# Seven products of sums in the up-projection of a diffusion-transformer layer's MLP

## The chip, the cores and the metric

The kernel runs on one core of a Trainium2 chip. The metric is the device time of one launch in microseconds (us). Engines are called as in the profile: PE (TensorE: matmuls), PEld (its weight loads), DVE (VectorE), ACT (ScalarE), POOL (GpSimd), SP (SyncE, which issues nearly all DMAs of this kernel).

## The reference, cut to what matters

One layer over 2048 tokens of width 1024: modulated norm, input projection, retention and grouped attention side by side, output projection, then an MLP with a squared ReLU, and a final norm.

```python
h = _modulate(_rmsnorm(x, norm1_g), sh1, sc1)
...
x = x + g1 * (jnp.concatenate([ret, att], axis=-1) @ w_out)
h2 = _modulate(_rmsnorm(x, norm2_g), sh2, sc2)
x = x + g2 * (jnp.square(jax.nn.relu(h2 @ w_ff1)) @ w_ff2)
...
return _rmsnorm(x, final_norm_g)
```

`h2` is 2048 x 1024, `w_ff1` 1024 x 4096, `w_ff2` 4096 x 1024, all in 32-bit floats. The change is in how `h2 @ w_ff1` (the up-projection) is computed.

## The kernel before, in words

**Three stages.** First the projections of the normed input, in an order that a scheduler chooses at build time; at the end of this stage `ff_scales` works out powers of two by which weights and activations of the MLP are scaled. Then attention, with retention and the output projection woven into it. Then the MLP, called feed-forward here. Attention and feed-forward are ordered by hand: attention is a list of numbered steps, each with phases ("scores", "exp", "late", "dma" and so on), and `on(k, phase, fn)` puts a call into step k. There are 18 steps for each of 32 groups of attention. Within each engine the instructions run in the order in which they were called, and so do the DMAs of SP.

**16-bit halves.** In feed-forward every operand is held as two 16-bit floats, hi and lo: ACT writes hi as a cast, DVE (or POOL) writes lo as the difference (`split16`, and the same with a scale in `make_piece`). A product of two such operands takes three matmuls: hi by hi, hi by lo, lo by hi.

**The output tiles.** `output_tile(t, ...)` adds the output projection of token tile t (128 tokens) to x, stores the row (`x1_d`), norms it, transposes it and stores the modulated, transposed tile of `h2` in DRAM (`h2_d[t]`: 128 partitions x 8 slices of the width x 128 tokens). The tiles come from the last token to the first, one per 24 steps; the last one or two end after attention.

**Feed-forward.** The 2048 tokens are taken in two halves (`halves`) of 8 tiles. For each half the 4096 hidden columns are taken in 16 blocks of 256, so there are 32 blocks. A block has two parts:
- Up: 4 tiles (two slices f of 128 hidden columns by two groups tg of 512 tokens). A tile is 8 slices of the width x 3 matmuls of 128 x 128 by 512, into one of four PSUM banks (`up_part`). `up_out` then takes it: ReLU with scale (ACT), square (POOL), hi (ACT), lo (DVE).
- Down: 16 tiles (8 token tiles m by two slices n of 512 columns), each of 2 x 3 matmuls (`down`); DVE adds each to the row `acc` of its token tile. There are four banks for these, two pools of two, taken by turns: m even and m odd; in the first block only one pool.

The weights of a block come in pieces of 256 KB (`fetch_piece`) and are split, w2 after a multiplication by the gate g2 on POOL (`make_piece`), one block ahead. The h2 of a half stays in SBUF as hi and lo: `fetch_h` reads 16 pieces, `make_h` splits them. `prelude` puts this for the first half, and the up tiles of block 0, into the last steps of attention. At the turn between the halves, block 15's down tiles are interleaved with the second half's splits, and with the squares, roots, final scaling and stores of the first half's rows, for which the second half's rows are then loaded (`ending`, steps kept in the list `rest`).

Of the kernel before, what the change touches and what calls it, by code (L numbers as in the profile page):

```python
# [54 lines left out]
def layer_kernel(ctx: ExitStack, tc: tile.TileContext, a: dict, out: bass.AP):  # L55
# [43 lines left out]
    x1_d = scratch("x1", NT, [P, D])  # L99
    gate_d = [dram.tile([D], F32, name=f"gate{r}", tag=f"gate{r}") for r in range(2)]  # L100
# [12 lines left out]
    w2s = const.tile([P, 1], F32, name="w2s")  # L113
# [146 lines left out]
    with ExitStack() as st:  # L260
# [400 lines left out]
        def ff_scales():  # L661
# [3 lines left out]
            def spread():  # L665
                w = xp.tile([P, D], F32, name="fs", tag="x", bufs=6)
                x["m"], m = w[:, 4:516], w[:, :4]
                nc.vector.tensor_reduce(
# [11 lines left out]
            def scales():  # L680
                b = sm.tile([P, 8], F32, name="fsb", tag="fsb", bufs=1)
# [13 lines left out]
                nc.vector.tensor_scalar_mul(b[:, 6:7], b[:, 6:7], 8192.0)  # L695
# [4 lines left out]
                nc.vector.tensor_scalar_mul(sc1, sc1, 8192.0)  # L700
# [4 lines left out]
                nc.vector.scalar_tensor_tensor(scu, scu, 2.0**-26, b[:, 7:8], op0=ALU.mult, op1=ALU.mult)  # L705

                nc.vector.reciprocal(w2s, w2)
                nc.vector.tensor_scalar_mul(w2s, w2s, 8192.0)
# [211 lines left out]
    xp = pool(side, "wx", 2, side="right")  # L920
# [253 lines left out]
    def output_weights(k0):  # L1174
# [8 lines left out]
        def fetch(k, n):  # L1183
            w = xp.tile([P, 2, 512], F32, name="wos", tag="xr")
# [33 lines left out]
    def output_tile(t, k, direct, first, last):  # L1218
# [6 lines left out]
        def fetch_x():  # L1225
            y["x"] = xp.tile([P, D], F32, name="xr", tag="xr")
            nc.sync.dma_start(y["x"], a["x"][0, t * P : (t + 1) * P, :])
# [102 lines left out]

    for i in range(3):
        on(18 + i, "begin", more_keys, 0, i)
        on(26 + 4 * i, "late", more_keys, 1, i)
    done = attention()
    k = output_weights(retention(24))
    for n, t in enumerate(range(NT - 1, -1, -1)):
# [4 lines left out]
        made_at, last = output_tile(t, k, n >= DIRECT, n == 0, n == NT - 1)  # L1341

# [5 lines left out]
    halves = [list(range(NT - 1, NT // 2 - 1, -1)), list(range(NT // 2 - 1, -1, -1))]  # L1348
    ff = {}
    w1, w2 = {}, {}  # L1350
# [3 lines left out]
    def open_early():  # L1354
        attn.close()
        keep.close()
        ff["h"] = pool(early_ff, "fh")
        ff["w1"] = pool(early_ff, "fw", 6)
        ff["s"] = pool(early_ff, "fs", 5)
        ff["ps1"] = pool(early_ff, "fp1", 4, space=PSUM)  # L1360

    def open_late():
        room.close()
        ff["w2"] = pool(late_ff, "fw2", 3, side="right")
        ff["r"] = pool(late_ff, "fr", 2, side="right")
        ff["up"] = pool(late_ff, "fq", 6, side="right")
# [6 lines left out]
        nc.sync.dma_start(ff["g2"], gate_d[1].partition_broadcast(P))  # L1373

        m = one.tile([P, 4], F32, name="gm")
        e, r, k = (m[:, i : i + 1] for i in range(3))
        nc.vector.tensor_reduce(e, ff["g2"], axis=AX.X, op=ALU.max, apply_absolute_value=True)
        binade(e)
        nc.vector.tensor_scalar_mul(e, e, 2.0)
        nc.vector.reciprocal(r, e)  # L1380
        nc.vector.tensor_scalar_mul(r, r, w2s)
        nc.vector.tensor_scalar_mul(ff["g2"], ff["g2"], r)
        nc.vector.tensor_tensor(k, sc2, e, op=ALU.mult)
        ff["k"] = k
# [5 lines left out]
    def pieces(b):  # L1390
        return [(2, b, 1, 0), (2, b, 1, 1), (1, b + 1, 0), (1, b + 1, 1), (2, b + 1, 0, 0), (2, b + 1, 0, 1)] + [
            (1, b + 1, 2),
            (1, b + 1, 3),
        ]

    queue = [(1, 0, i) for i in range(4)] + [(2, 0, 0, n) for n in range(2)]
    for b in range(2 * NB):
        queue += [p for p in pieces(b) if p[1] < 2 * NB]
    fetched, made = [], []

    def fetch_piece():
        if len(fetched) == len(queue):
            return
        m, b, i, *n = queue[len(fetched)]
        f0 = b % NB * FB
        w = ff["s"].tile([P, 512], F32, name="ws", tag="ws")
        if m == 1:
            src = a["w_ff1"][0, 2 * i * P : (2 * i + 2) * P, f0 : f0 + FB]
            nc.sync.dma_start(w.rearrange("p (k n) -> p k n", k=2), src.rearrange("(k p) n -> p k n", p=P))
        else:  # L1410
            c = slice(n[0] * 512, (n[0] + 1) * 512)
            nc.sync.dma_start(w, a["w_ff2"][0, f0 + i * P : f0 + (i + 1) * P, c])
        fetched.append(w)

    def make_piece(ahead=2):
        if len(made) == len(queue):
            return
        while len(fetched) < min(len(made) + 1 + ahead, len(queue)):
            fetch_piece()
        m, b, i, *n = queue[len(made)]  # L1420
        w = fetched[len(made)]
        made.append(None)
        if m == 1:
            hi = ff["w1"].tile([P, 2, FB], F16, name="w1hi", tag="w1hi")
            lo = ff["w1"].tile([P, 2, FB], F16, name="w1lo", tag="w1lo")
            w1[b, i] = hi, lo
            w = w.rearrange("p (k n) -> p k n", k=2)
            nc.scalar.activation(hi, w, AF.Copy, scale=sc1)
            nc.vector.scalar_tensor_tensor(lo, w, sc1, hi, op0=ALU.mult, op1=ALU.subtract)
        else:  # L1430
            if n[0] == 0:
                w2[b, i] = [ff["w2"].tile([P, D], F16, name=f"w2{x}", tag=f"w2{x}") for x in ("hi", "lo")]
            c = slice(n[0] * 512, (n[0] + 1) * 512)
            hi, lo = w2[b, i]
            nc.gpsimd.tensor_tensor(w, w, ff["g2"][:, c], op=ALU.mult)
            split16(hi[:, c], lo[:, c], w)

    def new_h():
        ff["hs"] = [
            [ff["h"].tile([P, KT, 512], F16, name=f"h2{x}", tag=f"h2{x}{tg}") for x in ("hi", "lo")]  # L1440
            for tg in range(2)
        ]

    def fetch_h(hf, i):

        u = ff["u", i] = ff["s"].tile([P, 4, P], F32, name="u", tag="ws")
        nc.sync.dma_start(u, h2_d[halves[hf][i // 2]][:, i % 2 * 4 : i % 2 * 4 + 4])

    def make_h(i, eng=None):
        j, q = i // 2, i % 2  # L1450
        hi, lo = (x[:, 4 * q : 4 * q + 4, j % 4 * P : (j % 4 + 1) * P] for x in ff["hs"][j // 4])
        split16(hi, lo, ff.pop(("u", i)), eng or (nc.vector if i % 2 else nc.gpsimd))


    UP = [(f, tg) for tg in range(2) for f in range(NF)]
# [3 lines left out]
    def up_part(b, f, tg, k):  # L1459
        if k == 0:  # L1460
            pu[f, tg] = ff["ps1"].tile([P, 512], F32, name="pu", tag="pu")
        ps = pu[f, tg]
        whi, wlo = (x[:, k % 2, f * P : (f + 1) * P] for x in w1[b, k // 2])
        hi, lo = (x[:, k] for x in ff["hs"][tg])
        mm(ps, whi, hi, start=k == 0, stop=False)  # L1465
        mm(ps, whi, lo, start=False, stop=False)  # L1466
        mm(ps, wlo, hi, start=False, stop=k == KT - 1)  # L1467

    def up_out(f, tg):
        r = ff["r"].tile([P, 512], F32, name="r", tag="r")  # L1470
# [230 lines left out]
```

## Time and profile before

| | |
|---|---|
| median of 3 runs | 3048.44 us (3046.94 to 3048.74) |
| the profiled execution | 3047.53 us, span 3045.7 us |
| mean granted TensorE clock | 0.986 |
| PE busy, share of the span | 94% |
| DVE, ACT, POOL busy | 63%, 43%, 42% |
| DMA moved | 317.48 MB, mean 104 GB/s |
| feed-forward's matmuls (32 blocks x 192) | 6144 of 17524 |
| first up matmul, first down matmul, last down matmul start at | 1680.2, 1707.5, 3033.4 us |

The span is the time from the first to the last instruction of the profiled execution; its own time is a little longer. A stretch from A to B is counted in us from the span's start. Busy time of PE is the time in which at least one matmul was under way. In a timeline's row stand the start, the duration, engine, line, operation, the tiles written and read, the form, how many were merged, and in brackets the idle time of that engine just before, with what ended it.

### The profile page before, as it was taken

How to read it: one execution, taken by the hardware profiler on the slowest of the kernel's cores; microseconds unless marked ns; L12 is line 12 of the kernel's file. 1: busy time of each engine (PE TensorE's matmuls, PEld its weight loads, DVE VectorE, ACT ScalarE, POOL GpSimd, SP SyncE). 2: the span in 40 equal slices, each digit the busy share in tenths (PEclk: the TensorE clock that was granted, in tenths of full speed). 3: DMA queues.
4: the chain of work that ended last, by engine and by line, in shares of the span. 5: the costliest groups of instructions: out<-in, count | busy, mean ns of one | idle time of the engine just before them, and what ended most of it. 6: DMA issues, size and time to landing. Idle time of an engine off the chain costs nothing.

```text
span 3045.7 us, 45858 instructions
## 1 busy us (share of the span) xinstructions
PE 2874.4 (94%) x17524; PEld 1740.0 (57%) x17524; DVE 1932.4 (63%) x3035; ACT 1295.5 (43%) x2120; POOL 1271.7 (42%) x1046
## 2 busy tenths in 40 slices
PE   7999898998888799999998999999999999999998
PEld 3777787776666566666666444444444444444443
DVE  5889657449888977777775555554555555555455
ACT  2343334236667577777777322222223322222222
POOL 2536346236787655555555412222224321222222
PEclk9999999999999899999999999999999999999999
DMA  8988643435233212211112511111112411111111
GB/s 291 337 299 284 213 134 106 132 99 169 86 113 105 73 56 67 68 61 61 61 51 80 192 49 51 49 52 52 56 49 93 163 52 49 52 49 52 53 52 56
DMA packets 212116, 317.48 MB, mean 104 GB/s; under 512 B 49460, under 2 KB 110132, under 8 KB 211896
## 3 DMA queue, kind: packets, MB, share of 16 engines
q1 hardware_dynamic: 201616, 307.06, 30.5%
q10 hardware_dynamic: 10280, 7.48, 0.8%
q8 instruction: 138, 2.26, 0.3%
q14 instruction: 82, 0.67, 0.1%
HBM read 254.56 MB, written 59.91 MB: 103 GB/s over the span
## 4 chain that ended last, share of the span: by engine, by line
PE 69%; DVE 14%; DMA 6%; POOL 4%; issue 4%; ACT 2%; SPq 0%; ACTq 0%; DVEq 0%; POOLq 0%
PE pd L1482 7%; PE pd L1484 7%; PE pd L1483 7%; PE pu L1467 7%; PE pu L1465 7%; PE pu L1466 7%; PE o L229 3%; PE st L196 3%; PE st L195 3%; PE mp L158 3%; PE pso L789 3%; DVE nm L171 2%; PE pso L791 2%; PE pso L790 2%; PE bank L1250 2%
## 5 line engine op out<-in xcount | busy, mean ns | idle before, releaser
L1472 POOL TENSOR_TENSOR r<-r 128x512 f32<-128x512 f32 x128 | 134.5, 1051 | 942.2 <-ACT r L1471 942.2
L171 DVE TENSOR_REDUCE nm<-mp 128x1 f32<-128x512 f32 (+1 forms) x576 | 391.4, 685 | 210.9 <-PE mp L158 176.1
L1485 DVE SCALAR_TENSOR_TENSOR acc<-pd,gm,acc 128x512 f32<-128x512 f32 x512 | 373.7, 746 | 154.0 <-PE pd L1484 153.8
L212 POOL TENSOR_TENSOR plo<-p,phi 128x1024 f16<-128x1024 f32 x160 | 368.8, 2305 | 226.2 <-ACT phi L205 195.8
L201 ACT ACTIVATE p<-st 128x512 f32<-128x512 f32 x576 | 340.7, 598 | 249.2 <-PE st L196 174.5
L71 DVE TENSOR_TENSOR ulo<-r,uhi 128x512 f16<-128x512 f32 x128 | 111.4, 870 | 460.4 <-ACT uhi L70 460.4
L1482 PE MATMUL pd<-w2hi,uhi 128*128 128x512 f16 x1024 | 390.0, 381 | 14.1 <-DVE acc L1485 13.9
L1466 PE MATMUL pu<-h2lo,w1hi 128*128 128x512 f16 x1024 | 388.7, 380 | 2.6 <-POOL h2lo L71 2.6
L1465 PE MATMUL pu<-h2hi,w1hi 128*128 128x512 f16 x1024 | 388.9, 380 | 1.2 <-ACT h2hi L70 1.2
L1483 PE MATMUL pd<-w2lo,uhi 128*128 128x512 f16 x1024 | 389.9, 381 | 0.0
L1484 PE MATMUL pd<-w2hi,ulo 128*128 128x512 f16 x1024 | 389.7, 381 | 0.1
L1467 PE MATMUL pu<-h2hi,w1lo 128*128 128x512 f16 x1024 | 388.7, 380 | 0.0
L70 ACT ACTIVATE w2hi<-ws 128x512 f16<-128x512 f32 x128 | 77.4, 627 | 557.4 <-PE pd L1484 484.1
L789 PE MATMUL pso<-whi,hi_l 128*128 128x512 f32 (+1 forms) x768 | 295.1, 386 | 10.1 <-ACT xs L524 5.4
L205 ACT ACTIVATE phi<-p 128x1024 f16<-128x1024 f32 x288 | 303.7, 1055 | 0.0
L791 PE MATMUL pso<-whi,lo_l 128*128 128x512 f32 (+1 forms) x768 | 292.1, 381 | 3.3 <-DVE lo_l L67 3.3
L790 PE MATMUL pso<-wlo,hi_l 128*128 128x512 f32 (+1 forms) x768 | 291.5, 379 | 3.1 <-DVE wlo L67 3.1
L158 PE MATMUL mp<-ks,qr 128*128 128x512 f16 x512 | 196.7, 384 | 55.8 <-DVE nm L171 55.6
L229 PE MATMUL o<-wv,phi 128*128 128x129 f16 x2304 | 244.1, 221 | 0.0
L228 PE MATMUL o<-wv,plo 128*128 128x65 f16 x2304 | 237.2, 194 | 5.8 <-DVE plo L214 4.9
L228 PEld LDWEIGHTS <-plo 128*128 128x128 f16 x2304 | 203.1, 98 | 53.7 <-issue 37.5
L214 DVE TENSOR_TENSOR plo<-p,phi 128x512 f16<-128x512 f32 x256 | 214.4, 839 | 19.2 <-ACT phi L205 19.1
(357 smaller groups left out, 5409.2 us busy)
## 6 DMA issues: line engine op xcount, KB each, us to landing
ws<-in_w_ff SPq DMA_DIRECT2D x256, 256.0 KB, 2.7
wm<-in_w_ff SPq DMA_DIRECT2D x64, 512.0 KB, 5.5
wst<-in_w_in SPq DMA_DIRECT2D x60, 512.0 KB, 5.3
wst<-in_w_mod SPq DMA_DIRECT2D x32, 512.0 KB, 5.9
orv<-rv SPq DMA_DIRECT2D x35, 256.0 KB, 3.0
ork<-rk SPq DMA_DIRECT2D x34, 256.0 KB, 3.0
wst<-in_w_mod SPq DMA_DIRECT2D x32, 256.0 KB, 4.4
x_l<-in_x SPq DMA_DIRECT2D x16, 512.0 KB, 7.5
```

The lines of the kernel that those rows point to most:

```text
L171: nc.vector.tensor_reduce(dst, src, axis=AX.X, op=ALU.max, negate=True)
L212: nc.gpsimd.tensor_tensor(lo, p, hi, op=ALU.subtract)
L228: mm(o[:, : HD + 1], lo[:, i, c], v[:, : HD + 1], start=False, stop=False)
L789: mm(ps[:, :width], hi[:, k], wh, start=k == 0, stop=False)
L791: mm(ps[:, :width], lo[:, k], wh, start=False, stop=k == KT - 1)
L1465: mm(ps, whi, hi, start=k == 0, stop=False)
L1466: mm(ps, whi, lo, start=False, stop=False)
L1467: mm(ps, wlo, hi, start=False, stop=k == KT - 1)
L1482: mm(ps, uh, wh, start=f == 0, stop=False)
L1483: mm(ps, uh, wl, start=False, stop=False)
L1484: mm(ps, ul, wh, start=False, stop=f == NF - 1)
L1485: nc.vector.scalar_tensor_tensor(acc[:, c], ps, ff["k"], acc[:, c], op0=ALU.mult, op1=ALU.add)
```

## The change

**Seven products.** With the width cut in two halves (first and last four slices), the block's 256 columns in two slices f, and the 1024 tokens of a half in two groups tg, the up-projection of a block is a 2 x 2 by 2 x 2 block product. It is now computed as seven products of sums of blocks, each of 4 slices x 3 matmuls, and `up_out` puts the four tiles together from them as they come: product 0 is copied out of PSUM by ACT, each later one is added by DVE to a running sum in SBUF; after products 3, 4, 5 and 6 one of the four tiles is complete, and ReLU and square follow; `up_split` (hi, lo) of a tile is called one product later (`SPLIT_AFTER`), the last one after the first down tile.

**Weight forms.** `fetch_w1` reads a block's 1 MB of w1 in two DMAs into two 4 KB rows per partition, two blocks ahead. `sum_w1` makes four sums on POOL, `form_w1` splits seven forms (hi on ACT, lo on DVE) during the seven products of the block before (for block 1: during the first seven down tiles of block 0).

**h2 forms.** `h_pair` takes two token tiles (one of each tg), makes four differences on POOL, splits seven forms, and stores each in DRAM (`hf_d`), in runs of 256 bytes; a half has four such pairs. Those of the first half are put into the attention steps after output tiles 11 to 8, those of the second half between the down tiles with even m from block 1 on, one step each (52 in all). `fetch_h` reads the seven forms of a half, 1 MB each, in one DMA each.

**Order of the down tiles.** Outside of the turn and the last block, the four tiles of m = 6 and 7 of a block are kept back until after the next block's seven products (`LATE`).

**Scales.** The scaling of g2, before at the start of feed-forward, is done in `ff_scales` in the projection stage, and read back from DRAM (`gs_d`). The steps of the powers of two change with it.

The diff, cut to its core:

```diff
+    hf_d = [scratch(f"hf{i}", 7, [P, 2, 4, 512], F16) for i in range(2)]
+    gs_d = dram.tile([D], F32, name="gs", tag="gs")
...
+    def h_pair(hf, j):
+        x = {}
+        def fetch(g):
+            w = xp.tile([P, KT, P], F32, name="hb", tag="hb", bufs=2)
+            nc.sync.dma_start(w, h2_d[halves[hf][j + 4 * g]])
+            x[f"b1{g + 1}"], x[f"b2{g + 1}"] = w[:, :4], w[:, 4:]
+        def add(to, p, q, at=None):
+            x[to] = x[at] if at else xp.tile([P, 4, P], F32, name="hs", tag="hu", bufs=3)
+            nc.gpsimd.tensor_tensor(x[to], x[p], x[q], op=ALU.subtract)
+        def form(i, w):
+            f = xp.tile([P, 2, 4, P], F16, name="hp", tag="hp", bufs=2)
+            split16(f[:, 0], f[:, 1], x[w])
+            nc.sync.dma_start(hf_d[hf][i][:, :, :, j * P : (j + 1) * P], f)
...
+        if t in halves[0][4:]:
+            for i, step in enumerate(h_pair(0, 11 - t)):
+                on(last + 2 + 2 * i, "dma" if i < 2 else "late", step)
...
+    def form_w1(b, i):
+        w = w1[b, i] = ff["w1"].tile([P, 2, 4, P], F16, name="w1f", tag="w1f")
+        src = raw1[b, FORMS1[i]]
+        nc.scalar.activation(w[:, 0], src, AF.Copy, scale=sc1)
+        nc.vector.scalar_tensor_tensor(w[:, 1], src, sc1, w[:, 0], op0=ALU.mult, op1=ALU.subtract)
...
-    UP = [(f, tg) for tg in range(2) for f in range(NF)]
-    def up_part(b, f, tg, k):
+    def up_part(b, i, k):
         if k == 0:
-            pu[f, tg] = ff["ps1"].tile([P, 512], F32, name="pu", tag="pu")
-        ps = pu[f, tg]
-        whi, wlo = (x[:, k % 2, f * P : (f + 1) * P] for x in w1[b, k // 2])
-        hi, lo = (x[:, k] for x in ff["hs"][tg])
-        mm(ps, whi, hi, start=k == 0, stop=False)
-        mm(ps, whi, lo, start=False, stop=False)
-        mm(ps, wlo, hi, start=False, stop=k == KT - 1)
+            pu[i] = ff["ps1"].tile([P, 512], F32, name="pu", tag="pu")
+        whi, wlo = (w1[b, i][:, x, k] for x in range(2))
+        hi, lo = (hs[i][:, x, k] for x in range(2))
+        mm(pu[i], whi, hi, start=k == 0, stop=False)
+        mm(pu[i], whi, lo, start=False, stop=False)
+        mm(pu[i], wlo, hi, start=False, stop=k == 3)
...
-    def up_out(f, tg):
-        r = ff["r"].tile([P, 512], F32, name="r", tag="r")
-        nc.scalar.activation(r, pu.pop((f, tg)), AF.Relu, scale=scu)
+    def relu(f, tg):
+        r = rs[f, tg]
+        nc.scalar.activation(r, r, AF.Relu, scale=scu)
         nc.gpsimd.tensor_tensor(r, r, r, op=ALU.mult)
+    def up_out(i):
+        ps = pu.pop(i)
+        def add(to, x):
+            nc.vector.tensor_tensor(to, ps, x, op=ALU.add)
+            return to
+        if i == 0:
+            pu["v"] = new_r("v")
+            nc.scalar.activation(pu["v"], ps, AF.Copy)
+        elif i == 1:
+            pu["q"] = add(new_r("q"), pu["v"])
+        elif i == 2:
+            rs[1, 0] = add(new_r("w"), pu["q"])
+        elif i == 3:
+            rs[0, 0] = add(new_r("r"), pu["v"])
+            relu(0, 0)
+        elif i == 4:
+            pu["w"] = rs[1, 0]
+            rs[1, 0] = add(new_r("r"), pu["w"])
+            relu(1, 0)
+        elif i == 5:
+            rs[1, 1] = add(pu["w"], pu["w"])
+            relu(1, 1)
+            add(pu["q"], pu["q"])
+        elif i == 6:
+            rs[0, 1] = add(pu["q"], pu["q"])
+            relu(0, 1)
+    SPLIT_AFTER = {4: (0, 0), 5: (1, 0), 6: (1, 1), 7: (0, 1)}
...
+        pairs = [step for j in range(4) for step in h_pair(1, j)]
+        LATE = (6, 7)
         for b in range(2 * NB):
...
+            jobs = [("up", i) for i in range(7) if b]
+            if b % NB:
+                jobs += [("down", b - 1, m, n) for m in LATE for n in range(2)]
+            jobs += [("down", b, m, n) for m in range(NM) for n in range(2) if turn or final or m not in LATE]
             for i, (what, *at) in enumerate(jobs):
                 if what == "up":
+                    for k in range(4):
+                        up_part(b, i, k)
+                    up_out(i)
+                    if i in SPLIT_AFTER:
+                        up_split_of(b, *SPLIT_AFTER[i])
+                    if b < 2 * NB - 1:
+                        if i < 4:
+                            sum_w1(b + 1, *SUMS1[(0, 1, 2, 3)[i]])
+                        form_w1(b + 1, i)
+                    if turn:
+                        fetch_h(1, i)
...
+                bb, m, n = at
+                if b and i == 8:
+                    up_split_of(b, *SPLIT_AFTER[7])
+                down(bb, m, n, accs[m])
...
+                if pairs and b and m % 2 == 0:
+                    pairs.pop(0)()
```

More of the change, by code (lines that the diff above doesn't have):

```diff
@@ L1415, in make_piece, with fetch_w1 @@
[L1415 to L1420, printed above, removed]
+    raw1, w1, w2, hs = {}, {}, {}, {}
+    def fetch_w1(b):
+        f0 = b % NB * FB
+        for i in range(2):
+            w = xp.tile([P, D], F32, name="w1r", tag="xr", bufs=3).rearrange("p (k n) -> p k n", k=4)
+            src = a["w_ff1"][0, i * 512 : (i + 1) * 512, f0 : f0 + FB]
+            nc.sync.dma_start(w, src.rearrange("(k p) n -> p k n", p=P))
+            for j in range(2):
+                raw1[b, f"a{j + 1}{i + 1}"] = w[:, :, j * P : (j + 1) * P]
@@ new lines, in layer_kernel, with fetch_w2, make_w2 @@
+    queue2 = [(b, i, n) for b in range(2 * NB) for i in range(NF) for n in range(2)]
+    fetched, made = [], []
+    def fetch_w2():
+        if len(fetched) < len(queue2):
+            b, i, n = queue2[len(fetched)]
+            f0 = b % NB * FB
+            w = ff["s"].tile([P, 512], F32, name="ws", tag="ws")
+            c = slice(n * 512, (n + 1) * 512)
+            nc.sync.dma_start(w, a["w_ff2"][0, f0 + i * P : f0 + (i + 1) * P, c])
+            fetched.append(w)
+    def make_w2(ahead=2):
+        if len(made) == len(queue2):
+            return
+        while len(fetched) < min(len(made) + 1 + ahead, len(queue2)):
+            fetch_w2()
+        b, i, n = queue2[len(made)]
```

218 lines of the change are left out of this document (85 added, 133 removed).

## The prediction

> **What bounds the kernel now.** I read the page first (span, shares), then the stretches of the span, then the instructions of the feed-forward stretch by form, then the timeline of single engines there.
>
> ```profile
> span 3045.7 us, 45858 instructions
> ## 1 busy us (share of the span) xinstructions
> PE 2874.4 (94%) x17524; PEld 1740.0 (57%) x17524; DVE 1932.4 (63%) x3035; ACT 1295.5 (43%) x2120; POOL 1271.7 (42%) x1046
> ...
> ```
>
> The profiled execution took 3047.53 us, 1.8 us more than its span; the median of the three runs shown is 3048.44, 0.9 us above it. The sum below is made against 3047.5. A measurement of this kernel tells about 0.2% (6 us) from no change.
>
> The page says TensorE; whether it has slack has to be read by stretch. Columns below: stretch, length, busy time and count of PE, PEld, DVE, ACT, POOL, then granted clock, DMA share, GB/s.
>
> ```profile
> 1300.00:1400.00 100.00, 98.33 (x872) 66.96 (x871) 72.02 (x124) 73.79 (x117) 54.06 (x35) 1.00 0.21 66
> 1680.00:1710.00 30.00, 26.15 (x113) 11.51 (x112) 14.81 (x23) 12.85 (x23) 16.27 (x15) 0.94 0.82 279
> 1790.00:2200.00 410.00, 410.00 (x1901) 185.89 (x1900) 208.49 (x279) 98.56 (x158) 95.60 (x77) 1.00 0.16 51
> 2337.00:2400.00 63.00, 52.35 (x221) 22.36 (x220) 39.12 (x44) 28.15 (x50) 35.48 (x30) 0.92 0.67 238
> 2400.00:3000.00 600.00, 600.00 (x2781) 272.01 (x2780) 304.51 (x406) 142.72 (x228) 140.39 (x113) 1.00 0.15 49
> ```
>
> In both long feed-forward stretches PE is busy to the last digit, with 600 us / 2781 = 0.2158 us for a matmul. A block has 96 up and 96 down matmuls: 192 x 0.2158 = 41.4 us. The ReLU of the last up tile comes back after just that (2002.60 and 2044.04 in the ACT rows below), so nothing but PE sets a block, and a matmul less is 0.2158 us less, for as long as the other engines keep up. The places where PE loses time are the stretch at 1680 (3.9 us idle), where feed-forward begins, and the turn between the halves of the sequence: 63.0 - 221 x 0.2158 = 15.3 us.
>
> **Part 1: the matmuls.** Seven products of 4 x 3 matmuls replace 4 tiles of 8 x 3: 84 for 96. Moving width (512) and weight shape stay. 32 blocks x 12 x 0.2158 = **-82.9 us**, if every block stays bound by PE.
>
> **Part 2: what the seven products leave for VectorE.** Before, a finished tile goes PSUM, ReLU (ACT), square (POOL), hi (ACT), lo (DVE), once in 5.2 us (24 x 0.2158). Now a product ends every 12 x 0.2158 = 2.59 us, and most need an add on DVE ahead of the ReLU; beside each product DVE also makes one of seven weight forms' low parts (four before). Durations (busy us, mean ns of one):
>
> ```profile
> L1485 DVE SCALAR_TENSOR_TENSOR acc<-pd,gm,acc 128x512 f32<-128x512 f32 x208 | 152.2, 746 | 66.4 <-PE pd L1484 66.4
> ...
> L1472 POOL TENSOR_TENSOR r<-r 128x512 f32<-128x512 f32 x53 | 55.0, 1038 | 410.6 <-ACT r L1471 410.6
> ...
> L1429 DVE SCALAR_TENSOR_TENSOR w1lo<-ws,sc,w1hi 128x512 f16<-128x512 f32 x52 | 37.6, 744 | 0.0
> L1471 ACT ACTIVATE r<-pu,scu 128x512 f32<-128x512 f32 x53 | 36.2, 682 | 113.8 <-PE pu L1467 113.8
> L1428 ACT ACTIVATE w1hi<-ws,sc 128x512 f16<-128x512 f32 x52 | 34.3, 706 | 0.0
> L70 ACT ACTIVATE uhi<-r 128x512 f16<-128x512 f32 x52 | 32.7, 630 | 59.7 <-POOL r L1472 59.7
> ```
> ```profile
> 1999.99 0.69 DVE L71 TENSOR_TENSOR ulo<-r,uhi 128x512 f16<-128x512 f32 x1 [1.66 <-ACT uhi L70]
> 2005.10 1.08 DVE L71 TENSOR_TENSOR ulo<-r,uhi 128x512 f16<-128x512 f32 x1 [4.42 <-ACT uhi L70]
> 2006.10 2.71 DVE L1485 SCALAR_TENSOR_TENSOR acc<-pd,gm,acc 128x512 f32<-128x512 f32 x4
> ```
> ```profile
> 2002.60 0.69 ACT L1471 ACTIVATE r<-pu,scu 128x512 f32<-128x512 f32 x1 [2.64 <-PE pu L1467]
> 2004.44 0.63 ACT L70 ACTIVATE uhi<-r 128x512 f16<-128x512 f32 x1 [1.15 <-POOL r L1472]
> ...
> 2044.04 0.69 ACT L1471 ACTIVATE r<-pu,scu 128x512 f32<-128x512 f32 x1 [2.64 <-PE pu L1467]
> ```
> ```profile
> 2003.37 1.04 POOL L1472 TENSOR_TENSOR r<-r 128x512 f32<-128x512 f32 x1 [4.07 <-ACT r L1471]
> 2004.37 2.94 POOL L1435 TENSOR_TENSOR ws<-ws,g2b 128x512 f32<-128x512 f32 x2
> ```
> ```profile
> 1678.59 0.68 DVE L1256 TENSOR_TENSOR xr<-bank,xr 128x512 f32<-128x512 f32 x1
> ```
>
> Total load is no worry: 7 adds, 7 form lows, 4 u lows, 16 evacuations and 4 w2 lows at about 0.7 are 27 us of DVE in 39. The order is. From the fifth product on, DVE's queue reads: add, u low of the tile before, form low, next add. ACT's reads: ReLU of this tile, u hi of the tile before, form hi. So the u low waits for a u hi that stands behind this product's ReLU, which waits for this product's add. One turn of that ring: add 0.69, about 0.08 to hand over, ReLU 0.61 until ACT takes the next (0.69 less a 0.08 overlap), u hi 0.63, 0.03, u low 0.60 to 0.99 (the 0.69 and 1.08 above, less overlap; the long one ran while POOL multiplied), form low 0.66: **3.30 to 3.69 us, against 2.59 that PE needs**. I take 3.45: POOL's square overlaps about half of the u low.
>
> Count from T, the end of the fifth product. Its add starts at about T+0.35 (0.2 to 0.5, behind the fourth product's form low). Three rings later, behind the sixth's and seventh's, the queue comes to the first down tile's evacuation: 0.35 + 3 x 3.45 + 0.75 = T+11.45. What PE does meanwhile: products six and seven, then the four down tiles kept back from the block before (they hide the last splits), into the four banks. The fifth down tile wants the first one's bank at 2 x 2.59 + 4 x 1.295 - 0.17 = T+10.19 (a down tile is 6 matmuls, 1.295 us; a matmul is shown 0.38 long though one starts each 0.2158, so an end is seen 0.17 after the next start). So PE waits **1.26 us** there (ends 0.66 and 2.13). Before, the same place has little room too: the last up tile is visible at 2002.57, DVE's u low stalls for u hi till 2005.10, the first evacuation ends at 2006.85, and the fifth down tile is due 4 x 1.295 - 0.17 = 5.01 later, at 2007.58. 30 blocks have this sequence: +37.8 us (0.66 gives 20, 2.13 gives 64; 0 if I have the order's effect wrong). After the stall DVE gains 1.295 - 0.66 a tile and is level by the next block.
>
> On the u low, the Trainium skill (SBUF — State Buffer, "Who interferes with whom") says that a VectorE instruction with two SBUF inputs and a GpSimd one exclude each other for the whole instruction. The rows show a share, not a lock: the u low at 2005.10 ended at 2006.18, while POOL's two multiplications were at work from 2004.37 to 2007.31. Had the first of them (half of 2.94, to 2005.84) kept it out, it would have ended no sooner than 2006.53. What a lock would give is rival B.
>
> **Part 3: forms of h2.** Each half has 4 pairs x 7 forms (hi on ACT, lo on DVE, one store) and 4 differences on POOL per pair. First half: inside attention, about 98 steps, some 160 us by my estimate. It adds 28 x 0.63 = 18 us ACT, 28 x 0.8 = 22 us DVE, 16 x 1.04 = 17 us POOL, lifting 74, 72 and 54% by 11 to 14 points; none reaches PE's 98%, but each form makes DVE wait for ACT in the middle of its maxima, on which PE waits. Taken at +3 (0 to 10). Second half: 52 steps, 8 a block, from block 1 on, between down tiles, right where DVE is behind; two buffers make a form wait for the store before last. The stores stand in SP's queue and wait there for DVE; behind them are q loads (first half) and w2 loads, both issued some tiles ahead. +1.5 us in 6.5 blocks, **+10** (0 to 26).
>
> **Part 4: start and turn.** The split of h2 (16 pieces a half) goes; instead seven tiles of 1.05 MB are read per half: 7.3 MB at 279 GB/s (row of 1680) is 26 us. At the start their products are spread over the last output tile's, so PE needs them at a pace of 4 us and is spared the 3.9 us idle; the last tile's x row now stands behind five of them in SP's queue, some 5 us late, and DVE with it, which the four up banks cover; but w2 still comes behind, and the first down tile needs u and w2, due about where it is now (1707.5, below). Block 0 has two down banks, and now seven forms beside its first seven tiles. Together **+2** (-5 to +10).
>
> ```profile
> L1482 PE MATMUL pd<-w2hi,uhi x1024: 376/379/634, 1707.5 to 3033.4; 128*128 128x512 f16 x171
> ```
>
> At the turn the loads go out as each product of the last block frees its tile, and 16 down tiles (20.7 us) and four late ones cover them. What stays is DVE finishing the first half's rows between evacuations, so of the 15.3 us I take off only **-4** (-9 to +3).
>
> ```profile
> 2354.79 0.58 PE L1482 MATMUL pd<-w2hi,uhi 128*128 128x512 f16 x1 [3.31 <-DVE acc L1485]
> ...
> 2360.59 0.38 PE L1482 MATMUL pd<-w2hi,uhi 128*128 128x512 f16 x1 [1.39 <-DVE acc L1485]
> ```
>
> These two rows show Part 2's wait as it exists now, PE idle until DVE empties a bank. The gate and scale work moved into the projection stage (one reduction, one scaling, a load, a store) lies beside its matmuls: +0.5 (0 to 3).
>
> **Sum.** -82.9 + 37.8 + 3 + 10 + 2 - 4 + 0.5 = -33.6: **3014 us**. Its own range, with the stall between 0.66 and about 1.6 and the smaller terms moving together, is 2990 to 3036.
>
> **Rivals.**
> A, DVE keeps up (overlaps I don't see): stall 0, second-half forms +3: -82.9 + 3 + 3 + 2 - 4 + 0.5 = -78, 2969 us. For it: DVE is at 51% in the row of 2400. Against: the ring is counted from rows.
> B, the ring is longer. If POOL's square locks the u low out until it ends (0.5 us later), the ring is 3.85, the stall 0.35 + 11.55 + 0.75 - 10.19 = 2.46, 30 of them 74 us; with the second half's forms at +20 the change is -82.9 + 74 + 20 + 3 + 2 - 4 + 0.5 = +13: **3060, slower**. It decides from a ring of about 3.8. This is the result of the skill's lock.
> C, the waits cool the clock. After the 3.31 us gap a matmul takes 0.58, after 1.39 us 0.38; so stalls of 1.3 should not. If they do, the turn's clock (0.92 over 63 us, 5 us for two episodes, 2.5 each) prices 30 of them at 75: 3089. The Trainium skill (TensorE: Matmul & The Clock Gate, "A second HAM failure mode: psum-queue depth-cycling") warns of just such short idles between groups; the 0.38 row speaks against it here.
> D, the 7.3 MB are not hidden: 26 us against the 18.1 of 84 matmuls, 8 us at either end, and no gain at the turn: about 3034.
>
> **How the numbers follow.** Forecast 0.52, A 0.20, B 0.15, C 0.05, D 0.08. Predicted 3014. The range 2968 to 3050 takes in A's value, D and the part of B near break-even; some 0.08 lies below it and 0.12 above. Faster by over 0.2%: forecast, A and D, 0.80. B's short end gives 0.04 within 0.2% and C 0.01: 0.05. Slower: 0.15.
>
> **What would show it.** Right: matmul count down by 384; last ReLUs of successive blocks some 40.1 us apart (38.9 under A, over 41.4 under B); one PE gap a block of about 1.3 us ahead of the fifth down tile, released by DVE's accumulation; DVE's adds at 3.4 to 3.5 us in products five to seven; larger gaps in blocks 1 to 7. Attention's end within 10 us of now. Wrong: no gaps, gaps released by a DMA, or matmuls of 0.58 after each gap.

## The result, and the profile after

| | before | after |
|---|---|---|
| median of 4 runs, same chip | 3047.69 us | 3137.59 us (3136.97 to 3138.87) |
| the profiled execution's span | 3045.7 us | 3136.2 us |
| mean granted TensorE clock | 0.986 | 0.971 |

The changed kernel is slower: ratio 1.0296 (95% interval 1.0278 to 1.0314). The forecast was 3014 us, its range ended at 3050; the measured time is 88 us beyond that. Medians leave out one run of experiment 8 (5785.31 us) and two of experiment 12 (8578.34 and 13887.15 us), slow ones at a granted clock of 1.0 whose cause stays open. (DVE is VectorE, POOL is GpSimd, ACT is ScalarE.) On the page of after 384 matmuls are indeed gone, and PE's share of the span has fallen all the same:

```profile
span 3136.2 us, 45423 instructions
PE 2841.7 (91%) x17140; PEld 1710.7 (55%) x17140; DVE 2233.8 (71%) x3399; ACT 1388.2 (44%) x2272; POOL 1487.9 (47%) x1182
...
L1541 PE MATMUL pd<-w2hi,uhi 128*128 128x512 f16 x1024 | 405.1, 396 | 115.5 <-DVE acc L1544 105.0
```

PE waits 105 us for VectorE's evacuations ahead of down tiles. The stretches that the prediction read as "PE busy to the last digit", and the stretch of attention with the first half's h2 forms, after (stretch, length, then PE, PEld, DVE, ACT, POOL, clock, DMA share, GB/s):

```profile
1270.00:1450.00 180.00, 161.95 (x1393) 107.89 (x1392) 156.00 (x228) 133.94 (x219) 114.97 (x75) 1.00 0.42 123
1790.00:2200.00 410.00, 377.86 (x1680) 167.11 (x1680) 299.79 (x388) 129.70 (x211) 176.94 (x130) 0.96 0.26 79
2470.00:3077.00 607.00, 562.58 (x2517) 249.53 (x2516) 401.91 (x533) 176.15 (x280) 217.66 (x165) 0.97 0.14 46
```

Feed-forward has idle time and a clock below 1. The same amount of attention, counted by matmuls, before:

```profile
1270.00:1432.00 162.00, 158.71 (x1390) 107.39 (x1389) 118.71 (x201) 119.00 (x191) 89.09 (x58) 1.00 0.22 69
```

So 1390 matmuls of attention take 180 us where they took 162, with VectorE 37 us busier.

**A block.** Blocks (first up matmul to the next block's) took 41.44 us before, away from the start and the turn. After, in the second half of the tokens, they take 43.8 to 44.0 in most cases and 42.48 in four of fourteen (in the first half 42.4 to 44.1, and 47.4 in block 3); 180 x 0.2158 would be 38.85. PE's rows at the fifth down tile of the block that begins at 2469.7:

```profile
2492.84 0.38 PE L1543 MATMUL pd<-w2hi,ulo 128*128 128x512 f16 x1
2496.31 0.38 PE L1541 MATMUL pd<-w2hi,uhi 128*128 128x512 f16 x1 [3.09 <-DVE acc L1544]
2496.52 0.49 PE L1542 MATMUL pd<-w2lo,uhi 128*128 128x512 f16 x1
2496.81 0.63 PE L1543 MATMUL pd<-w2hi,ulo 128*128 128x512 f16 x1
2497.23 0.63 PE L1541 MATMUL pd<-w2hi,uhi 128*128 128x512 f16 x1
2497.66 0.63 PE L1542 MATMUL pd<-w2lo,uhi 128*128 128x512 f16 x1
```

It is the one gap that was forecast, at the place and with the releaser forecast, and 3.25 us long (start to start, less 0.2158; the bracket shows 3.09 since a matmul's end is seen late), not 1.26. Behind it some eight matmuls start 0.43 us apart: the clock has halved (its record is in the last section), 1.6 us more. In a block of 42.48 us the same gap is followed by full speed:

```profile
2583.88 0.38 PE L1541 MATMUL pd<-w2hi,uhi 128*128 128x512 f16 x1 [3.09 <-DVE acc L1544]
2584.10 0.38 PE L1542 MATMUL pd<-w2lo,uhi 128*128 128x512 f16 x1
2584.31 0.38 PE L1543 MATMUL pd<-w2hi,ulo 128*128 128x512 f16 x1
```

The chain that leads to this gap (start, length, what; "issue" is time in which the engine waits for nothing that the profile records):

```profile
2483.40 0.69 DVE r L1507
...
2485.45 0.65 DVE ulo L71
2486.09 0.39 issue
2486.48 0.74 DVE w1f L1441
2487.22 0.61 DVE w L1507
...
2490.91 0.61 DVE q L1507
...
2492.82 0.68 DVE ulo L71
2493.49 0.36 issue
2493.85 0.29 DVE w1f L1441
2494.14 1.38 issue
2495.52 0.75 DVE acc L1544
```

It is the ring of the prediction, add, ReLU, u high, u low, form low, but with unexplained time inside the u low (0.36 to 0.39) and 1.38 us inside the last form's low. GpSimd's rows, and the whole durations on VectorE, say what stands there:

```profile
2492.34 1.04 POOL L1496 TENSOR_TENSOR q<-q 128x512 f32<-128x512 f32 x1 [2.64 <-ACT q L1495]
2493.34 1.71 POOL L1468 TENSOR_TENSOR ws<-ws,g2b 128x512 f32<-128x512 f32 x1
```
```profile
2492.82 1.11 DVE L71 TENSOR_TENSOR ulo<-w,uhi 128x512 f16<-128x512 f32 x1 [1.31 <-ACT uhi L70]
2493.85 1.75 DVE L1441 SCALAR_TENSOR_TENSOR w1f<-w1s,sc,w1f 128x512 f16<-128x512 f32 x1
2495.52 0.74 DVE L1544 SCALAR_TENSOR_TENSOR acc<-pd,sc,acc 128x512 f32<-128x512 f32 x1
```

The square ends at 2493.38, and the u low 0.55 later; the multiplication, which could start at 2493.34, ends at 2495.05, 1.12 after the u low (begun with no low of VectorE running, it takes 1.27); the form's low ends another 0.55 later (alone it takes 0.74). Each waits for the other to finish. The evacuation, which reads PSUM, takes its plain 0.74 although GpSimd goes on multiplying.

**Where the 90 us are**, on the profiled executions, from the starts of matmuls and of attention's exponentials:

| part | forecast | measured |
|---|---|---|
| 384 matmuls fewer | -82.9 | -82.9 |
| waits in blocks 1 to 15 and 17 to 30 (gaps 102, slow matmuls 35) | +47.8 | +137.5 |
| attention with the first half's h2 forms | +3 | +19.0 |
| start of feed-forward, block 0 | +2 | +19.4 |
| turn | -4 | -5.6 |
| projection, last block | +0.5 | +2.8 |
| sum | -33.6 | +90 |

So of the 124 us by which the forecast missed, the length of the gaps is 54, the slow matmuls 35, the start 17 and attention 16.

### The profile page after: what moved, and what is told of

Same layout as the page of the kernel before. It is cut to its first block, busy times and chain, and to the rows that moved or that the text cites. A ratio compares the mean times of both kernels' runs of the same rounds, so it can differ in the third digit from the quotient of the medians.

```text
span 3136.2 us, 45423 instructions
## 1 busy us (share of the span) xinstructions
PE 2841.7 (91%) x17140; PEld 1710.7 (55%) x17140; DVE 2233.8 (71%) x3399; ACT 1388.2 (44%) x2272; POOL 1487.9 (47%) x1182
## 4 chain that ended last, share of the span: by engine, by line
PE 32%; DVE 11%; ACT 5%; issue 4%; POOL 1%; DMA 1%; SPq 0%; ACTq 0%; DVEq 0%; POOLq 0%
PE pd L1541 5%; PE pd L1542 5%; PE pd L1543 5%; PE pu L1486 3%; PE pu L1484 3%; PE pu L1485 3%; DVE w1f L1441 3%; DVE ulo L71 3%; ACT uhi L70 2%; DVE acc L1544 1%; DVE r L1507 1%; PE o L231 1%; PE st L197 1%; PE st L198 1%; PE bank L1259 1%
## 5 line engine op out<-in xcount | busy, mean ns | idle before, releaser
L1541 PE MATMUL pd<-w2hi,uhi 128*128 128x512 f16 x1024 | 405.1, 396 | 115.5 <-DVE acc L1544 105.0
L1544 DVE SCALAR_TENSOR_TENSOR acc<-pd,sc,acc 128x512 f32<-128x512 f32 x512 | 371.2, 744 | 93.4 <-PE pd L1543 93.2
L1542 PE MATMUL pd<-w2lo,uhi 128*128 128x512 f16 x1024 | 404.7, 395 | 4.6 <-DVE w2lo L71 4.6
L1543 PE MATMUL pd<-w2hi,ulo 128*128 128x512 f16 x1024 | 404.0, 395 | 2.3 <-DVE ulo L71 2.3
L1496 POOL TENSOR_TENSOR r<-r 128x512 f32<-128x512 f32 x64 | 66.5, 1039 | 583.8 <-ACT r L1495 583.2
L1484 PE MATMUL pu<-hf,w1f 128*128 128x512 f16 x896 | 340.3, 380 | 0.0
L1485 PE MATMUL pu<-hf,w1f 128*128 128x512 f16 x896 | 340.0, 379 | 0.0
L1486 PE MATMUL pu<-hf,w1f 128*128 128x512 f16 x896 | 339.9, 379 | 0.0
L216 DVE TENSOR_TENSOR plo<-p,phi 128x512 f16<-128x512 f32 x256 | 226.7, 887 | 18.8 <-ACT phi L207 18.7
L1542 PEld LDWEIGHTS <-uhi 128*128 128x128 f16 x1024 | 102.9, 100 | 244.2 <-issue 137.2
L1468 POOL TENSOR_TENSOR ws<-ws,g2b 128x512 f32<-128x512 f32 x128 | 198.0, 1569 | 63.6 <-DMA ws<-in_w_ff 63.6
```

What stands on the lines that cost most here:

```text
L1484: mm(pu[i], whi, hi, start=k == 0, stop=False)
L1485: mm(pu[i], whi, lo, start=False, stop=False)
L1486: mm(pu[i], wlo, hi, start=False, stop=k == 3)
L1541: mm(ps, uh, wh, start=f == 0, stop=False)
L1542: mm(ps, uh, wl, start=False, stop=False)
L1543: mm(ps, ul, wh, start=False, stop=f == NF - 1)
```

## Experiments

Two theories for the blocks. "Order": VectorE's queue between the fifth add and the first evacuation is what the fifth down tile waits for. "Port": VectorE is slow there only because GpSimd works beside it. Times are medians; ratios are to the kernel before, on the same chip.

**1. The last three weight forms moved to the down tiles** (4 to 6, where VectorE has time).

```diff
-                        form_w1(b + 1, i)
+                        if i < 4:
+                            form_w1(b + 1, i)
...
+                if 0 < b < 2 * NB - 1 and bb == b and n == 0 and 2 <= m <= 4:
+                    form_w1(b + 1, m + 2)
```

> The forms 4 to 6 of the next block's up weights are made beside the block's own down tiles 2 to 4 instead of beside products 5 to 7; nothing else changes. Theory 'order': VectorE's queue between the fifth add and the first evacuation is what makes the fifth down tile wait; the three low parts take 0.66, 0.66 and 1.67 us of it, so the 3.25 us gap shrinks to about 0.3 us, too short to cool the clock: 29 blocks that lose 137.5 us now lose about 13, time 3013 us (2995 to 3030). Rival 'port': VectorE is slow there because GpSimd works beside it, and whatever low part stands there is stretched; then only the plain 0.66 x 3 = 2.0 us go, a gap of 1.3 us stays: 3038 us.

3028.51 us, ratio 0.9935 (0.9912 to 0.9957). A steady block takes 39.49: the fifth tile's gap is gone, 0.6 us remain around the sixth, and in blocks 1 to 15 and 17 to 30 no matmuls at half speed follow one another. "Order" holds, and the 1.3 us that "port" would leave are not there. This one edit turns the loss into a gain.

**2. Only the last form moved.**

```diff
-                        form_w1(b + 1, i)
+                        if i < 6:
+                            form_w1(b + 1, i)
...
+                if 0 < b < 2 * NB - 1 and bb == b and n == 0 and m == 4:
+                    form_w1(b + 1, m + 2)
```

> Only the last of the seven forms (the one whose low part took 1.75 us) moves to the down tiles. Theory 'order', with a clock that does not cool in gaps below about 3 us: the gap goes from 3.25 to 1.6 us, the 8 matmuls at half speed go, 29 blocks lose 1.8 instead of 4.74 us: 3052 us (3040 to 3065). Rival 'every gap cools': the 1.6 us of slow matmuls stay behind the shorter gap: 3095 us. Rival 'port': the next low part (u low) is stretched in place of it, the gap stays at 2.2 to 3.25 us: 3065 to 3137 us.

3068.17 us (1.0060, 1.0041 to 1.0079), above the range of "order" and inside that of "port". But the gap is 1.58 us as "order" had it, not 2.2 or more; 0.38 more stand at the sixth tile, which I had left out (29 x 0.38 = 11 us of the 16 us miss; the rest stays open):

```profile
2462.18 0.38 PE L1543 MATMUL pd<-w2hi,ulo 128*128 128x512 f16 x1
2463.98 0.38 PE L1541 MATMUL pd<-w2hi,uhi 128*128 128x512 f16 x1 [1.42 <-DVE acc L1544]
2464.19 0.38 PE L1542 MATMUL pd<-w2lo,uhi 128*128 128x512 f16 x1
2464.41 0.38 PE L1543 MATMUL pd<-w2hi,ulo 128*128 128x512 f16 x1
```

Matmuls start 0.22 apart at once after it. After block 0 matmuls at half speed stand only in block 3, behind a gap of 5.2 us, and at the turn. So not every gap cools the clock.

**3. The second token group's splits moved behind own down tiles 0 and 1**, forms where they were.

```diff
-    SPLIT_AFTER = {4: (0, 0), 5: (1, 0), 6: (1, 1), 7: (0, 1)}
+    SPLIT_AFTER = {4: (0, 0), 5: (1, 0), 8: (1, 1), 9: (0, 1)}
...
+                if b and bb == b and m < 2 and n == 1:
+                    up_split_of(b, *SPLIT_AFTER[8 + m])
```

> The splits of the second half of the tokens (u of tiles 4 to 7, which no down tile reads before the ninth own one) move from products 7 and the second late tile to behind the own down tiles 0 and 1; forms stay where they are. Theory 'order': the u low of 1.11 us and the wait for its u high (0.9 us) ahead of the first evacuation go, but the last form's low part may still meet GpSimd's multiplications: gap 1.4 to 2.3 us, no cooling, 3050 us (3035 to 3075). Rival 'forms alone': the u lows hide in waits for the matmuls anyway, gap above 3 us: 3125 us or more.

3056.56 us (1.0023, 1.0013 to 1.0034), as expected; the gap is 1.58, and the clock stays up but in block 3 (a gap of 5.5 us) and at the turn. The late tiles do not read these splits, so the splits need not stand ahead of them.

**4. The multiplication of the down weights left out.**

```diff
-        nc.gpsimd.tensor_tensor(w, w, ff["g2"][:, c], op=ALU.mult)
```

> GpSimd's multiplication of the down weights by the scaled gate is left out, so the down weights are split unscaled; all else as after. Theory 'order': only the last form's low part gets its plain 0.74 us back from 1.75, gap 3.25 to 2.25 us, no cooling: 29 x 2.4 us less, 3068 us (3050 to 3085). Rival 'port': GpSimd's work beside VectorE is the whole cause; without the multiplications the gap is gone: 3000 us.

3121.53 us (1.0235, 1.0215 to 1.0254): neither. The gap stays at 3.25, for GpSimd's queue simply moves up, and a sum of weights now stands in the same place:

```profile
2477.98 1.71 POOL L1431 TENSOR_TENSOR w1s<-w1r 128x512 f32<-128x512 f32 x1
```
```profile
2478.49 1.75 DVE L1441 SCALAR_TENSOR_TENSOR w1f<-w1s,sc,w1f 128x512 f16<-128x512 f32 x1
...
3044.15 0.74 DVE L1441 SCALAR_TENSOR_TENSOR w1f<-w1s,sc,w1f 128x512 f16<-128x512 f32 x1
```

So GpSimd was at work beside the low all the same, and this run does not decide against "port". The second row of VectorE is in block 30, where no weights are left to sum: there the low takes 0.74, the gap is 2.25 instead of 3.25, and no matmul is slow. That is the 1.0 us of "order". Blocks 4, 7 and 15, where the low takes 0.74 too, have gaps of 2.13 to 2.25.

**5. The squares left out.**

```diff
-        nc.gpsimd.tensor_tensor(r, r, r, op=ALU.mult)
```

> After with the squares of the rectified up-projection left out (u is the rectified sum itself); forms, splits and multiplications stay where they are. Theory 'lock': a low part on VectorE, which reads two operands from SBUF, runs only when GpSimd's running instruction has ended, so the u low of 1.11 us is a wait of 0.42 for the square and the plain 0.69: without the square the adds of products 5 to 7 are 3.27 us apart instead of 3.69, the multiplications run earlier and the last low takes 0.74, the gap is 0.6 to 1.0 us, no cooling: 3023 us (3010 to 3040). Rival 'share': both only slow each other down while they overlap, and the multiplications, which now run earlier, still do so: lows at 0.9 to 1.3 us, gap about 2 us: 3070 us.

3048.07 us (1.0003, 0.9993 to 1.0012), outside the range of "lock" and 22 us short of "share". In blocks 1, 2 and 5 the lock's forecast is met to the digit:

```profile
1763.73 0.68 DVE L1506 TENSOR_TENSOR r<-pu,w 128x512 f32<-128x512 f32 x1
1765.72 0.69 DVE L71 TENSOR_TENSOR ulo<-r,uhi 128x512 f16<-128x512 f32 x1 [1.31 <-ACT uhi L70]
1766.33 0.75 DVE L1441 SCALAR_TENSOR_TENSOR w1f<-w1r,sc,w1f 128x512 f16<-128x512 f32 x1
1767.00 0.68 DVE L1506 TENSOR_TENSOR w<-pu,w 128x512 f32<-128x512 f32 x1
```

The u low takes 0.69, adds are 3.27 apart (before 3.69), the gap is 0.62. In later blocks the squares no longer hold GpSimd's queue back, its multiplications and sums drift beside other lows, and most blocks lose 1.5 to 2.4 us, 0.67 of it at the sixth tile: with the 6.2 us of block 3 that is about the 25 us more than expected.

**6. Forms and late splits together** (edits of 1 and 3).

> The forms 4 to 6 beside own down tiles 2 to 4 and the splits of the second half of the tokens behind own down tiles 0 and 1, together. Theory 'order': neither stands before the first evacuation any more, the wait of the fifth down tile is gone, a steady block takes 180 x 0.2159 = 38.9 us against 39.5 with the forms alone: 3008 us (3000 to 3018) where the forms alone gave 3028. Rival 'load': with three forms, two u lows and four low parts of the down weights VectorE has no room beside 16 evacuations, and the wait comes back at a later down tile: 39.5 us a block or more, 3027 us.

3003.94 us (0.9859, 0.9844 to 0.9874). A steady block takes 38.85 us, and PE is never idle there (blocks 3 and 4 together lose 3.6 us):

```profile
2400.00:2944.00 544.00, 544.00 (x2523) 246.62 (x2521) 395.52 (x538) 175.77 (x280) 205.51 (x165) 1.00 0.16 51
```

**7 to 9. Attention.** On top of 6: the steps of the first half's h2 forms 4 apart instead of 2 (`both_att4`), then also their low parts on GpSimd (`both_att4p`), then the low parts on GpSimd, but 2 apart (`both_att2p`).

```diff
-                on(last + 2 + 2 * i, "dma" if i < 2 else "late", step)
+                on(free + 4 * i, "dma" if i < 2 else "late", step)
+            free += 4 * 13
...
-            split16(f[:, 0], f[:, 1], x[w])
+            split16(f[:, 0], f[:, 1], x[w], nc.gpsimd if hf == 0 else nc.vector)
```

> As the last, and in attention the steps that make the forms of h2 for the first half stand 4 steps apart, one pair after the other, instead of 2. From exponential 330 to the last, attention took 391.9 us before and 410.9 after. Theory 'density': the loss comes where VectorE is over 85% busy and falls by more than half when the same work is spread over twice the time: 399 us for that stretch, 12 us less in all, 2996 us. Rival 'price a form': each form costs the same wherever it stands (19 us / 28 = 0.7 us): 411 us and no change against the kernel without it, 3008 us.

> As the last, and the low parts of the first half's h2 forms are made by GpSimd instead of VectorE. Theory 'VectorE': what PE waits for in attention is the maxima, which stand behind the low parts of 0.7 to 2.0 us: without these 394 us for the stretch from exponential 330, 2991 us. Rival 'GpSimd': its own low parts of the probabilities (2.3 us each) come late in turn, exponentials wait for their buffers: 405 us or more, over 3002 us.

> As 'both', with the low parts of the first half's h2 forms made by GpSimd, the steps 2 apart as in after. The stretch from exponential 330 took 410.5 us with VectorE's lows 2 apart, 406.7 with VectorE's 4 apart, 397.3 with GpSimd's 4 apart. Theory 'VectorE': the engine decides, the spacing adds its 4 us: 401 us, 2996 us. Rival 'density of GpSimd': 28 more instructions on GpSimd in 160 us, which is busy two thirds of it, hold its own low parts of the probabilities up: 408 us, 3002 us.

| | exponential 330 to the last | median | ratio |
|---|---|---|---|
| before | 391.9 us | | |
| 6: VectorE, 2 apart | 410.5 | 3003.94 us | 0.9859 (0.9844 to 0.9874) |
| VectorE, 4 apart | 406.7 | 3001.77 | 0.9852 (0.9837 to 0.9867) |
| GpSimd, 4 apart | 397.3 | 2993.62 | 0.9822 (0.9806 to 0.9838) |
| GpSimd, 2 apart | 410.2 | 3000.99 | 0.9853 (0.9829 to 0.9877) |

The medians carry some 5 us of earlier stages; the stretch itself is the better measure. Neither edit alone does much (3.8 and 0.3 us), both together save 13. What PE waits for, from 1267 to 1437, in 6, and then with GpSimd's lows 2 apart (who waits for whom: us, times, longest):

```profile
PE mp L160 <- DVE nm L173: 6.6, 9, 1.3
PE bank L1259 <- DVE xr L1265: 3.4, 3, 1.3
PE bank L1290 <- POOL xr L1285: 2.8, 2, 1.4
```
```profile
PE bank L1290 <- POOL xr L1285: 8.5, 4, 3.1
PE mp L160 <- DVE nm L173: 3.0, 4, 1.9
```

The maxima's wait halves, and one for GpSimd's norm of the rows takes its place. With GpSimd's lows 4 apart, in the same stretch, these two waits are 1.0 and 2.6 us. So I read the table thus: at 2 steps whichever engine gets the lows is too full; at 4 steps GpSimd has room. "Density" (399 us) is wrong for VectorE, where "price a form" (411) is nearer to 406.7; "VectorE" is nearly right at 4 steps (394 against 397.3) and wrong at 2 (401 against 410.2), where the rival "density of GpSimd" (408) holds.

**10. The start**, on top of 6: at block 0 splits first, then the down weights' pieces in the order in which they are read; and the second half's h2 steps beside own down tiles only.

```diff
+    queue2[1:3] = queue2[2:0:-1]
...
-            on(k1 + (6, 8, 15, 17)[i], "late", make_w2, 0)
+            on(max(k1 + 6, k0 + 5 + 3 * 7), "late", make_w2, 0)
...
-                if pairs and b and m % 2 == 0:
+                if pairs and b and bb == b and m % 2 == 0:
```

> As 'both', and around block 0: the four pieces of down weights are made only after the last product's sum (first the two that the first down tile reads), the first half's splits directly ahead of them, the second half's behind own down tiles 0 and 1; the second half's h2 steps stand beside own down tiles only. Theory 'queue': at the start VectorE's last sum stood 3.2 us behind a low part that waited for GpSimd's multiplication, and u behind that; the first down tile comes some 4 us earlier and its stalls for low parts shrink by 2, blocks 3 and 4 lose 2 to 3 us less: 2996 us (2990 to 3000). Rival 'data': the down weights themselves come late, block 0 stays at 67 us: 3001 us.

3005.21 us (0.9859, 0.9842 to 0.9877), no faster than 6. In the traces block 0 falls from 67.1 to 61.5 us as expected: VectorE's last sum starts at 1724.55, where in 6 it stood behind a low that waited for a multiplication, to 1727.17:

```profile
1726.56 0.69 DVE L71 TENSOR_TENSOR w2lo<-ws,w2hi 128x512 f16<-128x512 f32 x1 [3.19 <-ACT w2hi L70]
1727.17 0.68 DVE L1507 TENSOR_TENSOR q<-pu,q 128x512 f32<-128x512 f32 x1
```

But block 3 takes 46.0 us, for a difference on GpSimd now follows its load at once, and the down weights stand behind it; blocks 3 and 4 lose 3.6 us more than in 6, and the turn 1.2:

```profile
1873.21 1.26 POOL L1355 TENSOR_TENSOR hs<-hb 128x512 f32<-128x512 f32 x1 [12.73 <-DMA hb<-h]
```

**11 and 12. All together**, with the h2 steps beside own down tiles (`all4p`), and where after has them (`all4q`).

> All edits together: forms and splits beside down tiles, GpSimd's lows 4 steps apart in attention, the reordered start, the h2 steps beside own down tiles. If the gains add up: 2994 (forms, splits and GpSimd's lows 4 apart) less 8 for start and h2 steps: 2986 us (2980 to 2992).

> As 'all4p', but the second half's h2 steps stand where after has them, beside the late tiles too. With the steps beside own down tiles alone, block 3 took 46.2 us: a difference on GpSimd stood 12.7 us for the row loaded only two tiles earlier, with a multiplication of down weights behind it; in 'both' blocks 3 and 4 together take 81.3 us against 85.1. So 3.8 us less than 'all4p', 2985 us (2981 to 2990); if the load is as late here, 2989 us.

2989.28 us (0.9806, 0.9790 to 0.9821) and 2985.42 us (0.9790, 0.9776 to 0.9804), both inside their ranges; their intervals overlap, so that the second is faster is not shown by the times alone, though its blocks 3 and 4 take 80.0 us against 85.1. It is the best version found: 63 us less than before and 152 less than the change as made, with the same matmuls.

## Why the prediction was wrong, point by point

- **Part 1, matmuls: right.** 384 fewer, and 0.2158 us each is what they are worth once nothing else binds (38.85 us a block in 6).
- **Part 2, the ring: right in place and mechanism, too small by 2.0 us.** From the end of product five (the matmul that starts at 2482.48 in the trace of after, seen until 2482.86) the first evacuation ends at T+13.40, against T+11.45. Piece by piece: the fifth add at T+0.54 instead of 0.35 (+0.19); two rings of 3.74 and 3.69 instead of 3.45 (+0.53); the third up to its form low 3.02 instead of 2.79 (+0.23); the last form low 1.67 instead of 0.66 (+1.01). Sum 1.96, and 1.26 + 1.96 is the gap of 3.25 within 0.03. (29 blocks have it, not 30.)
- **The step that failed is the price of a low part beside GpSimd.** I read "a share, not a lock" from one merged row: two multiplications in 2.94 us, cut in equal halves. Seen alone, the first of them before is

```profile
2004.37 1.27 POOL L1435 TENSOR_TENSOR ws<-ws,g2b 128x512 f32<-128x512 f32 x1
```

  It ended at 2005.63, and the u low of that place at 2006.18, 0.55 later, just as the lows of after end behind GpSimd's instructions. Even with the right end my test would have failed, for it added the plain 0.69 behind it (2006.32). So the long value, 1.08, was what a low takes that starts with some 0.55 us of a GpSimd instruction left, not the upper end of a range. In after, in the steady blocks of the second half, the three u lows ahead of the first evacuation all start so beside a square and take 1.11, so no half should have been taken. Of the 1.96 us missed, 1.77 stand in the three rings and the last low, most of it in lows beside GpSimd. The Trainium skill (SBUF — State Buffer, "Who interferes with whom") states this lock; the trace agrees with it, and it was wrong to weigh it down.
- **What stands beside what was missed.** The last form's low was priced at 0.66 as if GpSimd were idle then. With the up-projection's squares done, its queue goes straight on to four multiplications. Experiment 4 shows that the place in its queue costs the 1.0 us, whichever instruction stands there.
- **Rival B** (chance 0.15) had the lock, and its ring of 3.85 was nearer to the measured 3.7 than my 3.45; with a gap of 2.46 it lacked the last low's 1.0 us.
- **Rival C** (0.05): its slow matmuls came, though not on its condition. "Stalls of 1.3 should not" cool the clock holds (1.5 us in experiments 2 and 3), but the stall was 3.25. Slow matmuls cost 35 us in all. The two failures multiply: a 2.0 us error in the gap cost 3.2 us a block.
- **Part 3, h2 forms.** The first half cost 19.0 us instead of 3. I compared shares with PE's 98% although PE waits for single maxima behind lows of up to 2 us. VectorE had 37 us more work instead of 22, and here too the rows show the lock: from exponential 330 on, 14 of the 28 new lows of after take their plain 0.67 to 0.69 us, the other 14, which start beside a GpSimd instruction, 0.79 to 2.02, 29.8 us in all; the lows of the probabilities on VectorE grow from 82.2 to 94.4 us. The maxima, which read PSUM, take 0.69 whatever GpSimd does. The second half cost less than its +10: blocks 1 to 7 took 3.4 us more than seven of the blocks 9 to 14 would.
- **Part 4.** The turn was right (-5.6). The start was not: +19.4 against +2. PE's waits of after from 1697 to 1765:

```profile
PE pd L1541 <- ACT uhi L70: 7.6, 1, 7.6
PE pd L1541 <- DVE acc L1544: 5.4, 3, 2.9
PE pd L1542 <- DVE w2lo L71: 4.6, 1, 4.6
```

  I had "the first down tile wants u and w2" with no price for the order in which one queue makes them. The order of a few calls is 5.6 us of it (experiment 10). Without the multiplications (experiment 4) block 0 takes 57.7 us instead of 66.9; the rest stays open.
- **Rivals A and D** did not occur: the gap was there, and no wait of PE at the start or the turn ends with a DMA.

## What to carry to other kernels

Saving matmuls pays only if the engines that serve them keep pace in the order in which their queues stand: follow one bank from the last product to its release, write down what every queue does in that window, and move what nobody needs yet out of it. Price a VectorE instruction with two SBUF operands by what GpSimd runs at that moment, from rows that stand alone. And check a gap against the clock: here a wait of 3.25 us mostly cost half as much again.

## What the runs showed of the hardware

- **The lock.** The low parts on VectorE in after from 1790 us on read two operands from SBUF. Sorted by the time that GpSimd's instruction still had to run when they began: none, 0.72 us on average (261); about 0.4 us, 1.02 (30); about 0.6, 1.11 (132); about 1.2, 1.74 (39). So some 0.55 us are added to what GpSimd has left. The other eleven fit this but for one, which began 0.03 us behind a GpSimd instruction and took 0.67, while that one took 1.84. Evacuations and adds, which read one operand from PSUM, take 0.74 and 0.68 in every class. GpSimd's own sums, differences and multiplications grow from 1.27 to 1.71 in the same way when a low of VectorE still has 0.6 us to run (127 instructions). Its squares began beside no low and took 1.04.
- **The clock.** Gaps are start to start, less 0.2158. Of the 29 blocks of after with 3.1 us or more ahead of the fifth tile, 22 had a stretch of half clock behind it, 7 had none. Of the 56 blocks of experiments 2 and 3 with 1.5 to 1.6 us, none had; of six single gaps of 2.1 to 2.6 us in experiments 1 and 4, one had. What decides is not the length of the gap. The granted clock of the trace changes only on a grid of 3.413 us, which runs through each execution (all changes of a trace lie within 4 ns of it). Four steps of it around the gap at 2492.84 (stretch, length, PE, PEld, DVE, ACT, POOL, clock, DMA share, GB/s):

```profile
2489.84:2493.24 3.40, 3.38 (x16) 1.45 (x15) 2.09 (x4) 1.70 (x3) 0.90 (x1) 1.00 0.00 0
2493.25:2496.65 3.40, 0.34 (x2) 0.19 (x2) 3.40 (x4) 1.41 (x3) 3.40 (x3) 1.00 0.00 0
2496.66:2500.06 3.40, 3.40 (x10) 1.21 (x8) 3.25 (x5) 1.65 (x3) 3.40 (x4) 0.50 0.00 0
2500.07:2503.48 3.41, 3.41 (x17) 1.55 (x16) 1.61 (x3) 0.23 (x1) 3.28 (x3) 1.00 0.00 0
```

  In the feed-forward stage of all fourteen traces, every full-clock step in which PE sat idle for 2.13 us or more was followed by half clock (58 steps), and none with 1.0 to 2.11 us idle was (163). At 2.12, with six matmuls in the step, 3 of 18 were. So the gap of 3.25 us behind 2580.41 cooled nothing: an edge of the grid, at 2582.0, cut it in two, with 1.36 us idle in the step before and 2.12 in the one behind. A single gap below 2.1 us did not cool the clock in that stage of any trace. The Trainium skill (TensorE: Matmul & The Clock Gate, "Part 1: The HAM clock gate") gives a free-running window of about 3.4 us, with the drop after an idle one. The traces agree with the window and its length, but not with its having to be idle throughout: 2.13 of 3.41 us were enough.
